# Sample attention rebuilt: a half chunk's softmax inside the next one's keys, its selection penalty as a matmul, and z's tanh in a tile of its own

## The chip, the cores and the metric

The kernel runs on one core of one Trainium2 chip. The metric is device time in microseconds: 939.07 us is the median of three runs of the kernel before (937.36 to 939.32).

## The reference, cut to what matters

One step of a hybrid decoder layer: an input projection, a gated short convolution beside a three-branch sparse attention, and an output projection; once for a prompt of 1024 tokens and once for 8 sample tokens with 2048 cached positions each. All data is float32. The sample attention, which the change rebuilds, is `nsa_block` with one query per sequence:

```python
s_cmp = einsum('bqgnd,bcgd->bqgnc', q, kv_cmp[:, :, 0])          # 64 compressed blocks
p_cmp = masked_softmax(s_cmp, cmp_end <= qp)
o_cmp = einsum('bqgnc,bcgd->bqgnd', p_cmp, kv_cmp[:, :, 1])
imp   = p_cmp summed over the 4 heads of a group, pairs of blocks added
score = where(valid, imp + bonus, -inf)                          # 33 blocks of 64 rows
_, idx = lax.top_k(score, 16)
sel   = sel_blocks[bi, gi, idx]                                  # gathered key and value rows
p_slc = masked_softmax(einsum('bqgnd,bqgkd->bqgnk', q, sel[..., 0, :]), sel_pos <= q_pos)
o_slc = einsum('bqgnk,bqgkd->bqgnd', p_slc, sel[..., 1, :])
p_win = masked_softmax(einsum('bqgnd,bkgd->bqgnk', q, kv_win[:, :, 0]), m_win)   # last 512 rows
o_win = einsum('bqgnk,bkgd->bqgnd', p_win, kv_win[:, :, 1])
o = gate[..., 0:1] * o_cmp + gate[..., 1:2] * o_slc + gate[..., 2:3] * o_win
# mixer_output
attn_branch = o * silu(z_attn)
y = x + concatenate([b_gate * conv_y * silu(z_conv), attn_branch]) @ w_out
```

The kernel does not gather the selected rows. It scores all 2048 cached rows and adds a penalty of -1e30 to those of blocks that were not chosen.

## The kernel before, in words

Each float32 matrix product is made of two or three products on PE, of a value's rounded high part and the rest: `copy(ACT, h, x)` rounds and `sub(DVE or POOL, l, x, h)` takes the rest (these helpers are L75, L76 and L79, and most rows of a trace carry their lines).

After the input projections, two streams run side by side (`merge`, L30, called at L1463). The first is the prompt's attention (`attn_stream`) and then the output projection (`out_stream`: two halves of 512 columns, each of eight token tiles, each tile 24 products of 512 columns). The second is the convolution's projections, the loading of the output weights, the compression of the cached rows (`cmp_stream`: 16 gathers, four accumulations) and the sample attention (`sample_stream`). Each stream yields estimated costs, and `merge` goes on with the one that is behind; `SO = 1.9` stretches those of the output projection. What comes out is arranged once more when the program is built, so instructions of both streams alternate more finely than the yields. On the chip each engine works through its own list in that order.

The sample attention works in half chunks `(c, h)`: a chunk c is 512 rows of each sequence (c = 4 the window, 0 to 3 the cached rows), h is half of the eight sequences. Its parts:

- Preparation (L1072 to L1135): transposed queries into QA and QB, the new rows' keys and values, and their scores `seh`.
- Compressed branch (L1137 to L1153): scores of the compressed blocks, softmax in `Sc`, its scaling (L1150), and its sum over sequences, `im` (L1152). Then the importances on PE (L1155), the top 16 by two rounds of maximum and replacement (L1162, L1163), the penalty `pen` (L1165), and the compressed values (L1172 to L1193).
- `keys(c, h)` (L1198): for four sequences transposes of the keys (L1206), high and low parts `kh`, `kl`, and products into `s` (L1221, L1222), each one tile late.
- `values(c, h)` (L1226): the softmax of the half chunk first: sum of two parts of the scores (L1235), penalty (L1242), maximum (L1246 or L1250), minimum with the old one (L1251), correction (L1252) and exp (L1247 or L1253) with running sums (L1254). Then transposes of it (L1258), and for four sequences high and low parts of the values `vhl` and 16 products (L1278); the result is corrected and added (L1292).
- The loop at the end calls `keys` of the next half chunk, whole, and then `values` of this one.

Tiles `sd` of 512 KB hold keys and values of one sequence's chunk. There are nine; window tiles come by SP (L1090), cached ones by an indirect load from POOL (L1087), asked for when a tile's values have been used.

At the end `sample_half` (L1367) multiplies the sample's rows with the output weights: the convolution's half after each half of the columns, the attention's half when everything else is done, and a write of y_sample (L1431) closes the kernel.

`z_attn` (L695) makes z's SiLU for the prompt's attention, 128 tokens at a time, with its tanh in the buffer `acc` that the convolution uses too (L711).

Of the kernel before, what the change touches and what calls it, by code (L numbers as in the profile page):

```python
# [60 lines left out]
def hymba_step_kernel(ctx, tc, io):  # L61
# [624 lines left out]
    cu = cv.tile([128, 2 + NTOK], F32, name="cu")  # L686
    uo = cv.tile([128, 4, 16], F32, name="uo")
# [7 lines left out]
    def z_attn(a, n):  # L695
        t = cv.tile([128, 512], F32, name="acc")[:, :4 * n].rearrange("p (a c) -> p a c", a=4)
        silu2(mixA[:, :, a:a + n], mixA[:, :, a:a + n], t)

    def conv_use(kind, i, c, o, s):
# [7 lines left out]
        else:  # L707
# [3 lines left out]
            acc = cv.tile([128, 512], F32, name="acc")  # L711
# [15 lines left out]
    def conv_stream():  # L727
        yield from chan
        p = bank("mm")
        for i in range(4):  # L730
            PE.transpose(p[:10, i * 128:(i + 1) * 128], uo[:, i, :10], ident)
        ur = cv.tile([128, 512], F32, name="acc")[:10]
        copy(ACT, ur, p[:10])
        SP.dma_start(io["p_conv"].rearrange("l b r c -> (l b r) c"), ur[0:2])
        SP.dma_start(io["s_conv"].rearrange("l b r c -> (l b) r c")[:, 1, :], ur[2:10])
        yield 400
# [17 lines left out]
    def attn_stream():  # L754
# [147 lines left out]
        for ui, u in enumerate(units):  # L902
            o = [None]
            share = PACE[u[0]]
            if ui % 4 == 2 and u[0] < 7:
                z_attn(u[0] * 128 + 128, 128)
            elif ui == 3:
                z_attn(SEQ, 8)
# [5 lines left out]
            for br, P in ((1, P1), (2, P2)):  # L914
# [25 lines left out]
                if ui == 0 and br == 1:  # L940
                    z_attn(0, 128)
# [30 lines left out]
    def cmp_stream():  # L972
# [95 lines left out]

    def sample_stream():
        sp_ = ctx.enter_context(pool("smp", "right"))  # L1070
        small = sp_.tile([64, 112], F32, name="small")
        SP.dma_start(small, io["c_small"])  # L1072
        mext, bonus, Gsel = small[:, 0:8], small[:, 8:48], small[:, 48:112]
        QA = sp_.tile([128, 2, 8, 8], F32R, name="QA")
        QB = [sp_.tile([128, 32, 8], F32R, name=f"QB{h}") for h in range(2)]
        POOL.memset(f(QA), 0.0)
        ptz = [sp_.tile([128, 4, 32, 8], F32R, name=f"ptz{h}") for h in range(2)]
        for h in range(2):
            POOL.memset(f(QB[h]), 0.0)
            POOL.memset(f(ptz[h]), 0.0)  # L1080
# [14 lines left out]
        for _ in range(NSD):  # L1095
            load(*next(ahead))


        p = bank("pt")
        qg = sp_.tile([8, 4, 2, 64], F32, name="qg", tag="st")  # L1100
        copy(DVE, qg, q_s.rearrange("p (g h d) -> p h g d", g=2, h=4))
        for h in range(4):
            PE.transpose(p[:, h * 8:h * 8 + 8], qg[:, h].rearrange("p g d -> p (g d)"), ident[:8, :8])
        for g in range(2):
            q = slice(g * 64, g * 64 + 64)
            pv = p[q, :32].rearrange("p (h b) -> p b h", h=4)
            copy(ACT, QA[q, 0, :, g * 4:g * 4 + 4], pv)
            sub(DVE, QA[q, 1, :, g * 4:g * 4 + 4], pv, f(QA[q, 0, :, g * 4:g * 4 + 4]))
        for h in range(2):
            for i in range(2):  # L1110
                copy(DVE, QB[h][:, 4 * i:4 * i + 28:9, :], f(QA[:, i, 4 * h:4 * h + 4]))
        QAf = QA.rearrange("p i b r -> p (i b r)")
        yield 600

        p = bank("pt")
        for i in range(2):
            PE.transpose(p[:, i * 8:i * 8 + 8], srows[1 + i][:, 0:128], ident[:8, :8])
        kn = sp_.tile([128, 2, 16], F32R, name="kn")
        copy(ACT, kn[:, 0], p[:, :16])
        sub(DVE, kn[:, 1], p[:, :16], f(kn[:, 0]))  # L1120
        vn = sp_.tile([8, 2, 2, 128], F32R, name="vn")
        for i in range(2):
            copy(ACT, vn[:, i, 0], srows[1 + i][:, 128:256])
            sub(DVE, vn[:, i, 1], srows[1 + i][:, 128:256], f(vn[:, i, 0]))
        p = bank("pt")
        PE.matmul(p[:, :16], QAf, kn[:, 0], start=True, stop=False)
        PE.matmul(p[:, :16], QAf, kn[:, 1], start=False, stop=True)
        se = sp_.tile([64, 2, 8], F32, name="se")
        copy(ACT, se, p[64:128, :16].rearrange("p (i b) -> p i b", i=2))
        DVE.tensor_tensor(se, p[0:64, :16].rearrange("p (i b) -> p i b", i=2), se, OP.add)  # L1130
        DVE.tensor_tensor(se, se, mext[:, None, :].to_broadcast([64, 2, 8]), OP.add)
        seh = sp_.tile([32, 2, 2, 8], F32, name="seh")
        for h in range(2):
            copy(ACT, seh[:, h], se[32 * h:32 * h + 32])
        yield 600  # L1135
# [224 lines left out]
    def out_stream():  # L1360
# [65 lines left out]
        while 8 not in done:  # L1426
            yield None
# [97 lines left out]
```

## Time and profile before

| | |
|---|---|
| runs, median (lowest to highest) | 939.07 us (937.36 to 939.32) |
| profiled execution | 939.33 us, span 937.6 us |
| PE busy | 873.8 us, 93% of the span |
| DVE busy | 619.4 us, 66% |
| ACT busy | 556.0 us, 59% |
| POOL busy | 404.3 us, 43% |
| bytes moved by DMA | 82.24 MB, 88 GB/s on average |

PE multiplies matrices, DVE, ACT and POOL are the vector, scalar and GpSimd engines, SP issues most transfers. A row of a group of instructions names line, engine, operation, the tile written and the tiles read, their shapes and the count; then the busy time in us, the mean of one in ns, and the idle time of the engine before them with what ended it. In a row of the timeline the first two numbers are start and duration in us, and a bracket at the end holds the idle time before it and what ended that. The chain of waits puts 49% of the span on PE, 7% each on ACT and DVE, 3% on POOL.

### The profile page before, as it was taken

The page shows a single profiled execution, that of the slowest core. Times are in us where ns is not written, and L with a number is a line of the kernel's source. Part 1 is how long each engine was busy: PE and PEld are TensorE (multiplying, and loading weights), DVE is VectorE, ACT ScalarE, POOL GpSimd, SP SyncE. Part 2 cuts the span into 40 slices and gives each one's busy share as a digit, 9 for nine tenths or more (in the row PEclk, how much of TensorE's full clock was granted, in tenths as well). Part 3 has the DMA queues.
Part 4 walks back from the last instruction along what each step waited for, and adds up shares of the span by engine and source line. Part 5 has one row for each costly group of instructions (what it writes and reads, how often), then busy time and mean ns, then how long its engine had stood idle before and what let it go on. Part 6 is the DMA issues. An engine that isn't in the chain of part 4 may idle for free.

```text
span 937.6 us, 16976 instructions
## 1 busy us (share of the span) xinstructions
PE 873.8 (93%) x5789; PEld 783.2 (84%) x5789; DVE 619.4 (66%) x1714; ACT 556.0 (59%) x1495; POOL 404.3 (43%) x550
## 2 busy tenths in 40 slices
PE   7988999999899999999989999999679999798998
PEld 6888999999689889898979899998568888576765
DVE  5896734788655555856775686577745555877883
ACT  5764543733665655656556666576757666675761
POOL 4132340311454444444434444343455543477761
PEclk8999989999999999999999999999989999899999
DMA  7513331211011000000000100001495661857631
GB/s 246 154 57 95 95 114 35 80 57 31 6 30 34 24 23 24 23 24 23 13 12 23 24 23 1 23 2 44 127 302 182 214 214 47 314 179 226 214 102 47
DMA packets 57955, 82.24 MB, mean 88 GB/s; under 512 B 14470, under 2 KB 43086, under 8 KB 55692
## 3 DMA queue, kind: packets, MB, share of 16 engines
q1 hardware_dynamic: 50956, 47.60, 16.9%
q0 software_dynamic: 6912, 33.56, 10.6%
q8 instruction: 46, 0.75, 0.3%
q14 instruction: 41, 0.34, 0.1%
HBM read 74.24 MB, written 11.10 MB: 91 GB/s over the span
## 4 chain that ended last, share of the span: by engine, by line
PE 49%; ACT 7%; DVE 7%; POOL 3%; issue 3%; DMA 1%; ACTq 0%; DVEq 0%; POOLq 0%
PE o L880 7%; PE pt L870 5%; PE s L796 5%; PE mm L225 5%; PE mm L224 5%; PE mm L223 5%; POOL P L845 2%; ACT P L786 2%; PE mm L1407 1%; PE pt L999 1%; PE mm L1405 1%; PE mm L1406 1%; PE mm L1023 1%; ACT ph L75 1%; PE o L1278 1%
## 5 line engine op out<-in xcount | busy, mean ns | idle before, releaser
L223 PE MATMUL mm<-hH,wh 128*128 128x384 f32 (+1 forms) x480 | 157.9, 329 | 0.0
L225 PE MATMUL mm<-hH,wl 128*128 128x384 f32 (+1 forms) x480 | 155.7, 324 | 0.0
L224 PE MATMUL mm<-hL,wh 128*128 128x384 f32 (+1 forms) x480 | 155.1, 323 | 0.0
L786 ACT ACTIVATE P<-P,stat 128x640 f32<-128x640 f32 (+7 forms) x192 | 112.9, 590 | 37.4 <-DVE stat L784 36.8
L79 POOL TENSOR_TENSOR wl<-wraw,wh 128x256 fp32r<-128x256 f32 (+1 forms) x120 | 87.7, 749 | 106.2 <-ACT wh L75 96.8
L79 DVE TENSOR_TENSOR pl<-pt,ph 128x512 fp32r<-128x512 f32 (+1 forms) x164 | 102.4, 636 | 45.3 <-ACT ph L75 43.9
L75 ACT ACTIVATE ph<-pt 128x512 fp32r<-128x512 f32 (+1 forms) x164 | 88.3, 549 | 66.1 <-PE pt L870 65.5
L845 POOL TENSOR_SCALAR P<-P,stat,gates 128x640 f32<-128x640 f32 (+7 forms) x128 | 101.1, 800 | 55.8 <-DVE stat L836 52.7
L870 PE MATMUL pt<-ident,P 128*128 128x128 f32 x592 | 95.5, 278 | 6.4 <-POOL P L845 3.5
L796 PE MATMUL s<-k,q 128*128 128x320 f32 (+8 forms) x416 | 95.8, 334 | 3.7 <-DVE q L79 1.5
L208 PE MATMUL mm<-wh,hH 128*128 128x256 f32 (+1 forms) x320 | 93.5, 292 | 0.4 <-ACT hH L75 0.4
L209 PE MATMUL mm<-wl,hH 128*128 128x256 f32 (+1 forms) x320 | 93.2, 292 | 0.2
L210 PE MATMUL mm<-wh,hL 128*128 128x256 f32 (+1 forms) x320 | 93.0, 291 | 0.0
L223 PEld LDWEIGHTS mm<-hH,wh 128*128 128x128 f32 x480 | 91.9, 191 | 0.8 <-DVE mixC L693 0.6
L224 PEld LDWEIGHTS mm<-hL,wh 128*128 128x128 f32 x480 | 91.9, 191 | 0.1
L225 PEld LDWEIGHTS mm<-hH,wl 128*128 128x128 f32 x480 | 91.9, 192 | 0.1
L784 DVE CUSTOM_DVE_ANT_0 P<-s,mask 128x32 f32<-128x32 f32 (+8 forms) x160 | 70.9, 473 | 27.0 <-PE s L796 22.4
L870 PEld LDWEIGHTS pt<-ident,P 128*128 128x128 f32 x592 | 70.0, 140 | 19.9 <-POOL P L845 10.1
L880 PE MATMUL o<-ph,v 128*128 128x256 f32 x264 | 74.5, 301 | 3.6 <-ACT ph L75 3.0
L880 PE MATMUL o<-pl,v 128*128 128x256 f32 x264 | 73.3, 300 | 3.3 <-DVE pl L79 3.2
L796 PEld LDWEIGHTS s<-k,q 128*128 128x128 f32 x416 | 66.8, 190 | 8.1 <-DVE q L79 1.7
L841 POOL TENSOR_SCALAR P<-P,stat,gates 128x32 f32<-128x32 f32 x64 | 22.9, 370 | 94.4 <-DVE stat L836 76.4
(342 smaller groups left out, 2182.9 us busy)
## 6 DMA issues: line engine op xcount, KB each, us to landing
wraw<-in_w_in_dram SPq DMA_DIRECT2D x56, 256.0 KB
xt<-in_x_prompt_dram SPq DMA_DIRECT2D x8, 512.0 KB
wor<-in_w_out_dram SPq DMA_DIRECT2D x16, 256.0 KB
xr<-in_x_prompt_dram SPq DMA_DIRECT2D x16, 256.0 KB
out_y_prompt_dram<-xr SPq DMA_DIRECT2D x16, 256.0 KB
sd<-in_state_win_kv_dram SPq DMA_DIRECT2D x8, 512.0 KB
out_s_win_dram<-in_state_win_kv_dram SPq DMA_DIRECT2D x8, 511.0 KB
cwr<-in_cmp_w_dram SPq DMA_DIRECT2D x32, 64.0 KB
```

The costliest lines, as they stand in the source:

```text
L75: return ACT.activation(out, in_, AF.Copy)
L79: return eng.tensor_tensor(out, a, b, OP.subtract)
L208: PE.matmul(o[:, :n], hH[t // 3][:, k, s], wh, start=k == 0, stop=False)
L209: PE.matmul(o[:, :n], hH[t // 3][:, k, s], wl, start=False, stop=False)
L223: PE.matmul(o[:, :n], wh, hH[c][:, k], start=k == 0, stop=False)
L224: PE.matmul(o[:, :n], wh, hL[c][:, k], start=False, stop=False)
L225: PE.matmul(o[:, :n], wl, hH[c][:, k], start=False, stop=k == 7)
L786: return lambda: ACT.activation(P, P, AF.Exp, bias=stt[:, 0, c:c + 1], scale=-1.0, accum_out=stt[:, 1, c:c + 1])
L796: PE.matmul(s[:, a:b], q[:, i], k, start=first, stop=not first)
L845: POOL.tensor_scalar(P[:, i, :n], P[:, i, :n], stt[:, 2, c + i:c + i + 1], gates[:, qi, gt:gt + 1], op0=OP.mult, op1=OP.mult)
L870: PE.transpose(p[:, y * 256 + i * 128:y * 256 + i * 128 + 128], src[:, i], ident)
L880: PE.matmul(o[0][:, :256], v, X[:, y * 256:y * 256 + 256], start=br == 1 and x == 0 and y == 0 and X is h[0], stop=last and y + 1 == len(p ...
```

## The change

The change has these parts:

- `sample_start` is new: the preparation of queries, new rows and `seh` (now negated, with its minimum) runs inside the compression, after gathers 4, 7 and 10, in a pool of its own. POOL copies the queries there. Two tiles are new: `penx`, the penalty spread over a chunk, and `pick`, which selects half of its rows.
- Compressed branch: `im` is reduced before the scaling; ACT scales `im`, POOL scales `Sc` with sum and gate in one operation. The keys of the first half chunk come before the importances' product. The compressed values (`compressed`) come after the first half chunk's softmax.
- Keys: a product may now be two tiles late, with three buffers; the penalty of a selected chunk is added by one more product into `s`, `penx` by `pick` (L1191 of the kernel after).
- Softmax (`weigh`, new): sum, negation and maximum in one DVE operation; the corrections for both parts of the result and the running sum on ACT. It is called in the middle of the next half chunk's keys, after their second tile.
- Values: the correction and addition read the result from PSUM in one operation for both parts; the parts are added at the end.
- The end: the sample's output products are placed inside the second half of the output projection, two token tiles after the sample attention is done, or at the end if it is not. `SO` is 1.95. The first four weight pieces of the second half are split by POOL, not DVE.
- `z_attn` takes 64 tokens at a time and has a tile of its own, `zt`; `acc` is 384 wide instead of 512.

```diff
     def z_attn(a, n):
-        t = cv.tile([128, 512], F32, name="acc")[:, :4 * n].rearrange("p (a c) -> p a c", a=4)
+        t = zt[:, :4 * n].rearrange("p (a c) -> p a c", a=4)
...
-            if ui % 4 == 2 and u[0] < 7:
-                z_attn(u[0] * 128 + 128, 128)
-            elif ui == 3:
+            if ui % 4 > 1 and u[0] < 7:
+                z_attn(u[0] * 128 + ui % 2 * 64 + 128, 64)
+            elif ui == 1:
                 z_attn(SEQ, 8)
...
+        start = sample_start(cp)
         for n in range(16):
...
+            if n in (4, 7, 10):
+                next(start, None)
...
+                products(2)
+                if b % 4 == 1 and between:
+                    between()
                 yield 870
...
+            if b == 3 and c < 4:
+                PE.matmul(s[:64], pick[:, 64 - 64 * h:128 - 64 * h], penx, start=False, stop=True)
...
+        im = sp_.tile([64, 64], F32, name="im")
+        DVE.tensor_reduce(im, Sc.rearrange("p (b c) -> p c b", b=8), axis=AX, op=OP.add)
         DVE.tensor_scalar(stt[:, 1:2], stt[:, 1:2], 1e-30, None, op0=OP.max)
         DVE.reciprocal(stt[:, 2:3], stt[:, 1:2])
-        DVE.tensor_scalar(Sc, Sc, stt[:, 2:3], None, op0=OP.mult)
-        im = sp_.tile([64, 64], F32, name="im")
-        DVE.tensor_reduce(im, Sc.rearrange("p (b c) -> p c b", b=8), axis=AX, op=OP.add)
+        ACT.activation(im, im, AF.Copy, scale=stt[:, 2:3])
+        POOL.tensor_scalar(Sc, Sc, stt[:, 2:3], gr[:, 0:1], op0=OP.mult, op1=OP.mult)
         yield 450
+        yield from keys(*steps[0])
+        products(0)
...
-            DVE.tensor_tensor(Sb[:, :512], s[0:32], t, OP.add)
-                DVE.tensor_tensor(v, v, penh[:, h][:, None, :, None].to_broadcast([32, 4, 32, 4]), OP.add)
-                DVE.tensor_reduce(nm, Sb[:, :w], axis=AX, op=OP.max, negate=True)
+            DVE.tensor_tensor_reduce(Sb[:, :512], s[0:32], t, scale=-1.0, scalar=1e30, op0=OP.add, op1=OP.min, accum_out=nm)
...
                 DVE.tensor_tensor(nm, nm, old, OP.min)
-                ACT.activation(al, old, AF.Exp, bias=nm, scale=-1.0)
-                DVE.scalar_tensor_tensor(su, su, al, cs, op0=OP.mult, op1=OP.add)
+                for i in range(2):
+                    ACT.activation(fac[32 * i:32 * i + 32, h, br:br + 1], old, AF.Exp, bias=nm, scale=-1.0)
+                ACT.activation(su, su, AF.Identity, bias=cs, scale=fac[0:32, h, br:br + 1])
...
-                t = sp_.tile([32, 256], F32, name="ot")
-                rows_sum(o, t, 32)
-                DVE.scalar_tensor_tensor(acc[:, h, 1], acc[:, h, 1], al, t, op0=OP.mult, op1=OP.add)
+                DVE.scalar_tensor_tensor(a, a, fac[:, h, br:br + 1], o[:64, :256], op0=OP.mult, op1=OP.add)
...
         for i, u in enumerate(steps):
-            if i + 1 < len(steps):
-                yield from keys(*steps[i + 1])
-            yield from values(*u)
+            if 0 < i < len(steps) - 1:
+                got = []
+                yield from keys(*steps[i + 1], lambda u=u, got=got: got.append(weigh(*u)))
+                Sb = got[0]
+            else:
+                Sb = weigh(*u)
+                yield 100
+            if i == 0:
+                yield from compressed()
+            elif i + 1 == len(steps):
+                yield 4000
+            yield from values(*u, Sb)
...
-                    late.pop(0)()
+                    late.pop(0)(POOL)
...
-    SC, SO, SM2, SS = 1.0, 1.9, 1.0, 1.0
+    SC, SO, SM2, SS = 1.0, 1.95, 1.0, 1.0
```

How the lists of two engines change shows at three places. On PE at the sample stage's start, before, from the compressed scores (kcH, kcL) to the importances (`pt<-im`, L1155) and the first keys' products (`s<-kh`, `s<-kl`); `om` and `mm` are output tiles:

```order
L1138 MATMUL s<-kcH,QA 128x512
L1139 MATMUL s<-kcL,QA 128x512
L1206 MATMUL ptx<-ident,sd 128x128 x4
L1406 MATMUL om<-wol_10622,mh 128x512
L1407 MATMUL om<-woh_10621,ml 128x512
L1155 MATMUL pt<-im,small 64x64
L1173 MATMUL pt<-ident,Sb 128x64 x4
L1206 MATMUL pt<-ident,sd 128x128 x4
L1221 MATMUL s<-kh,QB_10378 64x512
```

And now, PE at the importances' product (L1216), from the third key tile's transposes (L1169) on:

```order
L1169 MATMUL ptx<-ident,sd 128x128 x4
L1187 MATMUL s<-kh,QB_9456 64x512
L1188 MATMUL s<-kl,QB_9456 64x512
L1465 MATMUL om<-wol_10714,mh 128x512
L1466 MATMUL om<-woh_10713,ml 128x512
L1187 MATMUL s<-kh,QB_9456 64x512
L1169 MATMUL pt<-ident,sd 128x128 x4
L1188 MATMUL s<-kl,QB_9456 64x512
L1216 MATMUL pt<-im,small 64x64
```

The importances' product moved from behind one key tile to behind four; the compressed scores (L1196, L1197) stand some 35 rows ahead of it.

On PE at the first values, before: from the transposes of the first softmax (`pt<-ident,Sb`) to the first selected chunk's keys:

```order
L1258 MATMUL pt<-ident,Sb 128x32 x4
L1265 MATMUL ptx<-ident,Sb 8x32
L1206 MATMUL pt<-ident,sd 128x128 x4
L1405 MATMUL om<-woh_9977,mh 128x512
L1406 MATMUL om<-wol_9978,mh 128x512
L1278 MATMUL o<-vhl,ptz_10381 64x256 x16
L1286 MATMUL o<-vn,pte 64x256
```

And now the same place, where `sd` at L1169 are tiles of the first selected chunk and L1315 the value products:

```order
L1187 MATMUL s<-kh,QB_9457 64x512
L1188 MATMUL s<-kl,QB_9457 64x512
L1302 MATMUL ptx<-ident,Sb 8x32
L1464 MATMUL om<-woh_10719,mh 128x512
L1247 MATMUL o<-vcHL,ptc 128x256 x4
L1169 MATMUL pt<-ident,sd 128x128 x8
L1169 MATMUL ptx<-ident,sd 128x128 x3
L1315 MATMUL o<-vhl,ptz_10448 64x256 x16
```

Eleven transposes instead of four stand ahead of the first sixteen value products.

On POOL at the sample stage's start, before: from the tiles cleared there (QA, QB, ptz) to the first indirect loads (`sd<-in_cache_slc_kv`):

```order
L1080 MEMSET ptz_10382 128x1024
L79 TENSOR_TENSOR ml<-mixA,mh 128x512
L79 TENSOR_TENSOR vhl<-sd,vhl 128x4x128 x2
L1169 TENSOR_SCALAR Sb<-Sb,gr 64x512
L1087 DMA sd<-in_cache_slc_kv_dram,idx_s 128x1024 x5
L79 TENSOR_TENSOR ml<-mixC,mh 128x512
```

And now, with the low parts of the output weights (`wol`) among them:

```order
L1159 MEMSET ptz_10449 128x1024
L79 TENSOR_TENSOR wol_10708<-wor,woh_10707 128x512
L79 TENSOR_TENSOR wol_10714<-wor,woh_10713 128x512
L79 TENSOR_TENSOR ml<-mixC,mh 128x512
L1211 TENSOR_SCALAR Sb<-Sb,cst_10459,gr 64x512
L79 TENSOR_TENSOR ml<-mixA,mh 128x512
L79 TENSOR_TENSOR vhl<-sd,vhl 128x4x128 x2
L1147 DMA sd<-in_cache_slc_kv_dram,idx_s 128x1024 x5
L79 TENSOR_TENSOR wol_10720<-wor,woh_10719 128x512
```

Two weight subtractions and one more of an output tile come ahead of the first indirect loads; the scaling of the softmax moved ahead of the value subtractions.

## Rows read from the trace of the kernel before

**Rows 1.** Busy us (count) by stretch: PE, PEld, DVE, ACT, POOL; clock, DMA share, GB/s.

```profile
240.00:648.00 408.00, 395.94 (x2655) 364.89 (x2656) 260.87 (x767) 251.35 (x707) 183.25 (x300) 1.00 0.08 19
702.00:796.00 94.00, 91.95 (x615) 80.54 (x615) 48.86 (x87) 63.54 (x123) 42.31 (x53) 1.00 0.50 169
796.00:812.00 16.00, 10.47 (x51) 6.72 (x50) 13.77 (x42) 8.79 (x26) 8.76 (x8) 0.79 0.85 320
812.00:850.00 38.00, 37.35 (x222) 27.13 (x220) 29.84 (x60) 28.09 (x59) 25.30 (x22) 1.00 0.61 210
850.00:870.00 20.00, 17.45 (x100) 13.22 (x99) 15.88 (x24) 12.07 (x26) 12.65 (x12) 0.91 0.64 210
870.00:913.00 43.00, 40.30 (x236) 31.00 (x235) 34.75 (x71) 29.78 (x64) 31.69 (x26) 1.00 0.49 162
913.00:933.00 20.00, 20.00 (x94) 14.03 (x92) 8.99 (x19) 3.22 (x9) 5.10 (x5) 1.00 0.14 53
```

**Rows 2.** The same view over two low clocks and the load's peak.

```profile
800.00:804.00 4.00, 2.24 (x10) 1.20 (x10) 3.96 (x14) 2.98 (x8) 0.89 (x1) 1.00 1.02 413
804.00:811.00 7.00, 3.79 (x16) 2.96 (x17) 5.05 (x17) 2.91 (x8) 6.20 (x6) 0.52 0.87 303
862.00:866.00 4.00, 4.00 (x15) 2.59 (x13) 1.15 (x3) 1.22 (x2) 0.09 (x2) 0.57 0.47 153
```

**Rows 3.** Waits of PE from 795 us on: us in total, times, longest.

```profile
PE pt L1155 <- DVE im L1152: 4.3, 1, 4.3
PE s L1222 <- DVE kl L79: 2.8, 3, 2.1
PE s L1221 <- ACT kh L75: 1.5, 1, 1.5
PE pt L1258 <- ACT Sb L1253: 0.8, 1, 0.8
```

**Rows 4.** Timeline of DVE and PE at the importances.

```profile
805.03 0.76 DVE L1150 TENSOR_SCALAR Sb<-Sb,cst 64x512 f32<-64x512 f32 x1
805.82 1.02 DVE L1152 TENSOR_REDUCE im<-Sb 64x64 f32<-64x512 f32 x1
806.89 0.47 PE L1155 MATMUL pt<-im,small 64*64 64x64 f32 x2 [4.30 <-DVE im L1152]
```

**Rows 5.** Timeline of DVE, POOL and PE around 860 us.

```profile
857.92 3.02 DVE L1254 SCALAR_TENSOR_TENSOR stats<-stats 32x1 f32<-32x1 f32 x1
858.42 1.30 POOL L79 TENSOR_TENSOR vhl<-sd,vhl 128x512 fp32r<-128x512 f32 x1
859.66 1.27 POOL L79 TENSOR_TENSOR ml<-mixC,mh 128x512 fp32r<-128x512 f32 x1
861.61 0.45 PE L1222 MATMUL s<-kl,QB 128*64 128x512 f32 x1 [2.14 <-DVE kl L79]
```

**Rows 6.** Groups of DVE, 795 to 938 us, by shape.

```profile
L1242 DVE TENSOR_TENSOR Sb<-Sb,penh 32x512 f32<-32x512 f32 x8 | 9.2, 1151 | 0.0
L1235 DVE TENSOR_TENSOR Sb<-s,st 32x512 f32<-32x512 f32 x10 | 6.8, 677 | 9.8 <-ACT st L75 9.8
L1254 DVE SCALAR_TENSOR_TENSOR stats<-stats 32x1 f32<-32x1 f32 x6 | 4.1, 680 | 0.0
```

**Rows 7.** Indirect loads of `sd` and POOL's subtractions: timeline, group, landing, durations.

```profile
807.79 1.05 POOL L1087 DMA_INDIRECT sd<-in_cache_slc_kv_dram,idx_s  x1 [0.17 <-issue]
L1087 POOL DMA_INDIRECT sd<-in_cache_slc_kv_dram,idx_s x32 | 33.9, 1061 | 8.4 <-issue 4.0 <-PE pt L1206 0.9 <-POOL vhl L79 0.8
DMA to landing us min/median/max: 5.1/5.6/6.9
L79 POOL TENSOR_TENSOR vhl<-sd,vhl x20: 1290/1308/2390, 803.1 to 912.5; 128x512 fp32r<-128x512 f32 x20
```

**Rows 8.** Timeline of SP at the end.

```profile
934.55 0.30 SPq L1431 DMA_DIRECT2D out_y_sample_dram<-y  x1
```

**Rows 9.** The tanh of z by the tile `acc`: count, ns min/median/max, first and last start.

```profile
L692 ACT ACTIVATE acc<-mixA x9: 230/622/632, 237.1 to 562.5; 128x512 f32<-128x512 f32 x8, 128x32 f32<-128x32 f32 x1
```

More of the change, by code (lines that the diff above doesn't have):

```diff
@@ L731, in conv_stream @@
             PE.transpose(p[:10, i * 128:(i + 1) * 128], uo[:, i, :10], ident)
[L732 to L735, printed above, removed]
+        for a in range(2):
+            c = slice(a * 256, a * 256 + 256)
+            ur = cv.tile([128, CH], F32, name="acc")[:10, :256] if a else zt[:10]
+            copy(ACT, ur, p[:10, c])
+            SP.dma_start(io["p_conv"].rearrange("l b r c -> (l b r) c")[:, c], ur[0:2])
+            SP.dma_start(io["s_conv"].rearrange("l b r c -> (l b) r c")[:, 1, c], ur[2:10])
         yield 400
@@ L1096, in sample_stream @@
             load(*next(ahead))
[L1099 to L1108, printed above, removed]
@@ L1109, in sample_stream @@
-        for h in range(2):
[L1110 to L1135, printed above, removed]
+        ptz = [sp_.tile([128, 4, 32, 8], F32R, name=f"ptz{h}") for h in range(2)]
+        for h in range(2):
+            POOL.memset(f(ptz[h]), 0.0)
+        sums, pend = {}, []
@@ new lines, in keys @@
+        def keys(c, h, between=None):
+            s = sums[c, h] = bank("s")
+            for b in range(4 * h, 4 * h + 4):
+                r = tiles[c, b].rearrange("p (t j c) -> p t j c", t=4, j=2)
+                p = bank("pt")
+                for t in range(4):
+                    PE.transpose(p[:, t * 128:(t + 1) * 128], r[:, t, 0], ident)
+                kh = sp_.tile([128, 512], F32R, name="kh", bufs=3)
+                kl = sp_.tile([128, 512], F32R, name="kl", bufs=3)
+                copy(ACT, kh, p)
+                sub(DVE, kl, p, f(kh))
+                pend.append((s, c, h, b % 4, kh, kl))
+                products(2)
+                if b % 4 == 1 and between:
+                    between()
+                yield 870
@@ new lines, in products, with product @@
+        def products(n):
+            while len(pend) > n:
+                product(*pend.pop(0))
+        def product(s, c, h, b, kh, kl):
+            q = QB[h][:, b * 8:(b + 1) * 8].rearrange("p i r -> p (i r)")
+            PE.matmul(s[:64], q, kh, start=b == 0, stop=False)
+            PE.matmul(s[:64], q, kl, start=False, stop=b == 3 and c == 4)
+            if b == 3 and c < 4:
+                PE.matmul(s[:64], pick[:, 64 - 64 * h:128 - 64 * h], penx, start=False, stop=True)
+        steps = [(c, h) for c in (4, 0, 1, 2, 3) for h in range(2)]
@@ L1165, in sample_stream @@
         DVE.tensor_scalar(pen, sc[:, 0:32], BIG / 10, BIG, op0=OP.is_gt, op1=OP.mult)
[L1166 to L1169 removed]
+        copy(ACT, penx[0:64].rearrange("p (t n r) -> p t n r", t=4, r=4),
+             pen[:, None, :, None].to_broadcast([64, 4, 32, 4]))
         yield 100
[L1171 to L1173 removed]
@@ L1383, in out_stream, with sample_end @@
             yield None
+        def sample_end():
+            for n in range(2):
+                sample_half(n, 1)
+                yield 1700
+            SP.dma_start(y_sample, y8)
         late = []
+        over = 0
         for n in range(2):
```

227 lines of the change are left out of this document (132 added, 95 removed).

## The prediction, made before the result was known

> **What bounds the kernel now.** I read the slices of the page first: PE is busy 93% of the span and its digit is 9 nearly everywhere, so the kernel is a queue of matmuls, and a change is worth what it takes out of PE's idle time or puts into its work. Next the busy time by stretch [rows 1], to find where PE is not full. The long attention and convolution stretch (240 to 648 us) has 12 us of idle PE in 408. The compression stretch (702 to 796) has 2.05 in 94. The sample attention that follows is worse: 5.53 idle of 16 at its start, then 0.65 of 38, 2.55 of 20 and 2.70 of 43; after 913 PE is full again with the last output tiles. So the stage that the change rebuilds holds 11.4 us of idle PE. Then the same view over the places where the clock digit falls [rows 2]: 804 to 811 ran at a mean 0.52 and 862 to 866 at 0.57. These follow the two longest idle times. Half clock costs only while PE works: 3.79 us busy at 0.52 would have taken about 2.0 at full, so 1.8 lost; 4.00 at 0.57 would have taken 2.3, so 1.7 lost. At stake in all: 5.5 + 1.8 = 7.3 at the start and 5.9 + 1.7 = 7.6 after it.
>
> Who ended the waits [rows 3]: 4.3 us for the reduced block importances (L1152), 2.8 for the low halves of the keys on DVE, 1.5 for their high halves on ACT, 0.8 for a finished softmax. Two of them explain themselves. L1155 stands in PE's list behind only a few products, while its operand comes through a scaling and a 1.02 us reduction on DVE [rows 4]; PE, which works its list in order, sat still. And the 2.14 us before 861.61 [rows 5]: a one-column operation, L1254, held DVE for 3.02 us, and the subtraction for the keys stood behind it. It ended when POOL's two subtractions, 858.42 to 860.93, ended; its six instances average 0.68 us, far above what one column needs.
>
> [...]
>
> **The change part by part.** The sum is made against the profiled execution, 939.33 us (span 937.6, 1.7 around it); the runs' median is 939.07.
>
> *Start of the sample stage, 7.3 at stake.* The queries' and new rows' preparation moves into compression, and the importances are reduced before the scaling, which goes to ACT and POOL. More important is the place: in PE's new list between the scores' last product and L1216 stand four tiles' transposes, six key products and 23 output products, where L1155 stood behind one tile and two output products. The 27 added wide products are 6.5 us at 0.24 each (priced below), and the scaling of 0.76 us [rows 4] is off the path: more than the 4.3 us. So this wait goes, and with it, I expect, the low clock. What is late next: in the new list eleven transposes of the first selected chunk stand ahead of sixteen value products. Their tiles come by POOL's indirect loads, issued after POOL's share of the first values, now with two weight subtractions ahead. A load takes 5.6 us from issue to landing and the next is issued about 1.06 + 8.4/32 = 1.3 us later [rows 7], so the third lands some 8 us after the first issue, at 807.79 before. PE has 88 instructions from the stage's beginning at 796 to there, at the 0.17 us of 870 to 913 (40.30 us for 236 [rows 1]) 15 us, so it gets there at 811, and the third tile lands at 807.8 + 2.6 + 5.6 = 816 if POOL keeps its time. Bounds: 0, since POOL's first load came behind the scaling that waited with PE and may come 4 us sooner; 5, if the two extra subtractions (1.3 us each, 2.4 at the worst [rows 7]) use that up. I take the middle, 2.4. Term: -7.3 + 2.4 = **-4.9**, bounds -7.3 and -2.3.
>
> *The half chunks, 7.6 at stake.* For each of the eight half chunks of selected keys DVE loses the penalty addition (L1242, 1.15 us), the separate maximum, a copy and L1254; addition, negation and maximum become one operation with one input in PSUM, priced by L1235 at 0.68 [rows 6]. Over ten half chunks DVE gives up 9.2 + 4.1 + the ten maxima (6.8, at L1235's 0.68 each) = 20 us, and some more with the value accumulation that now reads PSUM directly; ACT gets a few one-column operations. DVE was busy 80.5 of the 101 us from 812 to 913 [rows 1], so by this it falls to about 60%. The softmax now runs while the next keys' last two tiles are transposed, so PE has products to do meanwhile. Not all idle time goes: kh still waits for ACT, and each list is fixed in advance. I take two thirds: **-5.0**, bounds -7.6 and -2.5.
>
> *The penalty as a matmul.* Eight extra 64x512 products on PE. From 913 to 933 PE did 94 products in 20.00 us, that is 0.21, with some narrower ones among them; I take 0.24: **+1.9**. Nothing hides it, since PE is the bound; bounds 1.7 and 2.3.
>
> *Compression.* It takes eight small PE instructions with their POOL, ACT and DVE work, and loses filler: in the new order one of its four accumulations has only the eight products of a sample half beside it, where before it had a whole output tile. PE's total is not changed by that, but alone the chain gather, regroup, transpose, split, product may not fill PE. The trace shows no such stretch. Bounds: -1.0 (half of the 2.05 idle there) and +2.6 (the idle share of the worst neighbour, 2.55 of 20, over one accumulation of some 20 us). I take **+0.8**, nearer to the full stretch.
>
> *Weight pieces on POOL.* Four subtractions of 0.67 leave DVE; POOL was idle 26% to 45% of each stretch from 796 to 913 [rows 1], so the cost is the queueing counted at the start. 0 beyond that.
>
> *The end.* The sample's output products move ahead of the last two tiles. Before, after PE's last product came two additions of about 0.68 and a 32 KB write issued at 934.55 [rows 8]; now one addition, and a 256 KB write. At 413 GB/s [rows 2] the larger write needs 0.55 more. **-0.2**, bounds -0.7 and +0.5. PE keeps 48 products behind the sample's last result, so its final chain stays covered.
>
> *z's tanh.* Nine tanh of 0.62 us become seventeen, sixteen of them half as wide, and they no longer share the convolution's one buffer. ACT and DVE gain some 1 us each in 408 us in which they are busy 62% and 64% [rows 1, 9]; the waits that the shared buffer caused ended on those engines, not on PE. **0**, bounds -1.5 and +1.5.
>
> Sum: 939.3 - 4.9 - 5.0 + 1.9 + 0.8 - 0.2 = 931.9 us, 0.8% below the median. All low bounds together give 924, all high bounds 941.
>
> **The rivals.** *All of the idle time goes.* The DVE relief and the cover are enough to fill PE as it is filled from 913 on: 939.3 - 7.3 - 7.6 + 1.9 - 0.2 = 926. For it: DVE's load in [rows 1]; against it: the loads at the start and ACT, at 60% to 74% busy, which copies every tile twice.
>
> *The gain goes into the loads.* The first selected chunk is waited for in full (5 us), PE's clock falls again and takes 1.8, and with a faster stage each later chunk's tiles come 0.5 us late in eight half chunks: 939.3 - 4.9 - 5.0 + 1.9 + 0.8 - 0.2 + (5 - 2.4) + 1.8 + 4 = 940, no change. For it: an 8 us path from issue to the third landing; against it: after the start the DMA share is 0.49 to 0.64.
>
> *Slower: the softmax returns in front of the keys.* The transposes of a finished softmax now stand ahead of the next half chunk's last key products in PE's list, so a late softmax stops the keys as well. Small operations of its chain have moved onto ACT, where they queue behind the tile copies in order. Before, such a wait showed 0.8 us [rows 3]. If the eight half chunks that are weighed amid keys wait w each and the half chunk term is lost, the time is 939.3 - 4.9 + 1.9 + 0.8 - 0.2 + 8w: slower than before from w = 0.3, and 943 at 0.8. Against it: between the last product that a softmax needs and its transposes stand, in the new list, sixteen value products, sixteen transposes and some dozen wide products; the last alone are 2.9 us at 0.24, and the chain's three wide steps about 0.7 each, priced by L1235.
>
> *The rebuilt order elsewhere.* Every engine's list after 240 us is arranged anew, and 12 us of small waits there may come out 3 us either way; this is in the bounds.
>
> **How the numbers follow.** Forecast 931.9, own range 927 to 936: 0.60. All idle gone, 926: 0.17. Gain lost in the loads, 936 to 941: 0.13. Softmax in front of the keys, 941 to 945: 0.10. What this kernel's runs can tell apart is about 0.2%, 1.9 us. Faster takes the first two and a third of the loads' case, 0.81; same 0.08; slower 0.11. The range for 8 in 10 leaves out the lower half of the second case and the upper end of the others: 924.5 to 939.
>
> **What would show it.** Right: the wait at the importances is gone, no clock below full in the middle of the stage, DVE's busy time there down by over 20 us, and PE idle some 4 us instead of 11.4. A wait of PE for tiles of the first selected chunk, of 2 to 3 us, is the price I set; 5 or more with a low clock is the second rival. Waits before the softmax transposes in most half chunks are the third. Wrong at the root would be a longer compression stretch or idle time of PE in attention by more than 3 us.

## The result and the profile after

The changed kernel takes **943.3 us** (median of five runs, 942.98 to 945.13) against 939.07 for the kernel before (five runs, 936.58 to 940.38): ratio 1.0057, 95% interval 1.0039 to 1.0074. It is slower by 0.6%. The forecast was 931.9 with a range of 924.5 to 939.

The stage that was rebuilt runs from the last product of compression to the end. First the busy time of it in the kernel before, then in the changed one (columns as in [rows 1]):

```profile
795.70:937.60 141.90, 125.95 (x695) 92.35 (x695) 104.89 (x215) 82.24 (x182) 83.49 (x69) 0.96 0.52 179
```

```profile
797.20:941.30 144.10, 128.40 (x704) 94.76 (x704) 85.83 (x166) 85.66 (x195) 87.80 (x76) 0.99 0.52 175
```

VectorE was relieved as forecast: 104.9 to 85.8 us, 19.1 less. TensorE's idle time did not move: 141.9 - 125.95 = 15.95 us before, 144.1 - 128.4 = 15.7 after. It is also busy for longer, although the clock is higher. What it waits for is different. The waits of TensorE from 797 us on (us in total, times, longest), against [rows 3]:

```profile
PE s L1188 <- DVE kl L79: 6.4, 8, 2.1
PE s L1187 <- ACT kh L75: 2.3, 4, 1.4
PE o L1315 <- DVE ptz L79: 0.9, 1, 0.9
PE s L1187 <- ACT penx L75: 0.9, 1, 0.9
```

The 4.3 us for the importances are gone, as forecast. The waits for the keys' low halves `kl`, 2.8 us before, are now 6.4, although the engine that computes them has less to do. The reason stands in the timelines around the three longest: GpSimd, VectorE, and TensorE's wait that followed.

```profile
805.18 1.29 POOL L79 TENSOR_TENSOR ml<-mixA,mh 128x512 fp32r<-128x512 f32 x1
806.45 2.50 POOL L79 TENSOR_TENSOR vhl<-sd,vhl 128x512 fp32r<-128x512 f32 x2
806.30 3.19 DVE L79 TENSOR_TENSOR vhl<-sd,vhl 128x512 fp32r<-128x512 f32 x1
809.42 0.68 DVE L79 TENSOR_TENSOR kl<-ptx,kh 128x512 fp32r<-128x512 f32 x1
810.15 0.44 PE L1188 MATMUL s<-kl,QB 128*64 128x512 f32 x1 [2.11 <-DVE kl L79]
...
825.25 0.96 POOL L1147 DMA_INDIRECT sd<-in_cache_slc_kv_dram,idx_s  x1 [3.24 <-DVE acc L1358]
826.24 1.28 POOL L79 TENSOR_TENSOR vhl<-sd,vhl 128x512 fp32r<-128x512 f32 x1
825.60 2.48 DVE L79 TENSOR_TENSOR vhl<-sd,vhl 128x512 fp32r<-128x512 f32 x1 [0.36 <-ACT vhl L75]
828.73 0.44 PE L1188 MATMUL s<-kl,QB 128*64 128x512 f32 x1 [1.25 <-DVE kl L79]
...
845.30 0.94 POOL L1147 DMA_INDIRECT sd<-in_cache_slc_kv_dram,idx_s  x1 [0.30 <-issue]
846.26 2.52 POOL L79 TENSOR_TENSOR vhl<-sd,vhl 128x512 fp32r<-128x512 f32 x2
846.42 2.92 DVE L79 TENSOR_TENSOR vhl<-sd,vhl 128x512 fp32r<-128x512 f32 x1 [2.19 <-ACT vhl L75]
850.00 0.45 PE L1188 MATMUL s<-kl,QB 128*64 128x512 f32 x1 [1.00 <-DVE kl L79]
```

These are the subtractions for the values' low halves, which the code hands to VectorE and GpSimd in turn. With GpSimd free of subtractions one takes VectorE 0.67 to 0.69 us (e8 below). Here it takes 3.19, 2.48 and 2.92, and each time it ends some 0.55 us after GpSimd's run of work (809.49 against 808.95, 828.08 against 827.52, 849.34 against 848.78): each was held until that run was over. The keys' subtraction stands behind it in VectorE's list, and TensorE behind that: 2.11, 1.25 and 1.00 us. The second wait was followed by half clock:

```profile
830.00:833.50 3.50, 3.50 (x16) 3.06 (x15) 1.44 (x4) 2.09 (x4) 1.83 (x2) 0.51 0.81 255
```

One difference of the two traces lies ahead of the rebuilt stage. The changed kernel's attention starts at half clock for 10.3 us, the kernel before for 3.4, and every later point of attention is some 3 us later:

```profile
239.50:249.80 10.30, 9.15 (x31) 8.10 (x32) 5.95 (x31) 5.63 (x23) 2.69 (x6) 0.50 0.01 2
```

The change is not needed for it: e5, e15 and e17 below work through the same lists as the kernel before up to 680 us, and show 10.2, 6.8 and 6.8 us of it. The other kernels, faster ones among them, lie between 3.4 and 10.2 too.

### The profile page after: what moved, and what is told of

It reads as the page before. It is cut to its first block, busy times and chain, and to the rows that moved or that the text cites. A ratio compares the mean times of both kernels' runs of the same rounds, so it can differ in the third digit from the quotient of the medians.

```text
span 941.3 us, 16976 instructions
## 1 busy us (share of the span) xinstructions
PE 879.3 (93%) x5797; PEld 787.4 (84%) x5797; DVE 607.2 (65%) x1687; ACT 561.5 (60%) x1524; POOL 408.2 (43%) x559
## 4 chain that ended last, share of the span: by engine, by line
PE 46%; ACT 9%; DVE 7%; issue 3%; POOL 3%; DMA 2%; SPq 0%; ACTq 0%; DVEq 0%; POOLq 0%
PE o L883 7%; PE pt L873 5%; PE s L799 5%; PE mm L225 5%; PE mm L224 5%; PE mm L223 5%; ACT P L789 2%; PE pt L1002 1%; PE om L1026 1%; DMA wor<-in_w_out_dram 1%; ACT ph L75 1%; PE om L1464 1%; PE om L1466 1%; PE om L1465 1%; PE mm L1026 1%
```

## The experiments

Ratios are to the kernel before, timed beside it on the same chip, with a 95% interval.

**First four: which part.** The edits, in this order:

```
e1: the kernel before, with the change's lines of z_attn, conv_use's acc, conv_stream and attn_stream
e2: the changed kernel, with those lines as before
e3: -  sub((DVE, POOL)[b % 2], vhl[:, :, 1], v, f(vhl[:, :, 0]))
    +  sub(DVE, vhl[:, :, 1], v, f(vhl[:, :, 0]))
e4: -  late.pop(0)(POOL)
    +  late.pop(0)()
```

> The kernel before with only z's edit (tanh in a tile of its own, pieces of 64 and at other units, the conv rows copied out in two halves). Theory 1, the smaller pieces at the first unit hold TensorE at half clock longer (239.5 to 249.8 us in the trace after, 241.0 to 244.4 before, and every later marker of attention is 2.3 to 3.3 us late): about 942, with the half clock near 240 us lasting some 10 us again. Rival, how long the clock stays low there does not depend on z's pieces: 939, within 1.5.

> The changed kernel with z's edit undone. Theory 1: about 940 (943.3 less 3.3). Rival (not z): 943, within 1.5. In neither case more than 1 us of change after the last compressed row.

> The changed kernel with all the subtractions for the values' low halves on VectorE; before they alternate between VectorE and GpSimd. Theory 2, the stage's gain was lost where a VectorE subtraction with both inputs in SBUF ran beside GpSimd's (3.19 us at 806.30, 2.48 at 825.60, 2.92 at 846.42, instead of 0.68) and the keys' low halves stood behind it (TensorE idle 2.1 + 1.25 + 1.0 us and the half clock from 830.0 to 833.5, 1.7): these three go, 943.3 - 4.35 - 1.7 = 937, and no such subtraction is above 1.5 us except beside GpSimd's subtractions of the output's rows. Rival, VectorE gets 20 more subtractions of 0.68 = 13.6 us and the keys' low halves come late all the same: 943 or more.

> The changed kernel with the four weight pieces' subtractions back on VectorE. Theory 2: GpSimd reaches its two subtractions of the values about 3 us sooner, no longer together with VectorE's at 806.30, so the wait of 2.1 us at 810 shrinks or goes: 941 to 943. Rival, the weight pieces have no part in it: 943.3, within 1.

e1: 939.24, ratio 1.0003 (0.9985 to 1.0021), and its low clock lasted from 241.9 to 248.7 us. Theory 1 falls: z's edit costs nothing, to within 1.7 us. e2: 1.0040 (1.0024 to 1.0057), which overlaps the changed kernel's own interval.

e3: **933.57, ratio 0.9933** (0.9909 to 0.9957), nearly 10 us from one line. VectorE got 13.6 us of work (twenty subtractions at 0.68), and TensorE waits less for it. VectorE's busy time in the stage rose by only 1.05 us (86.88 against 85.83), so by estimate some 12.5 us of what counted as its busy time in the changed kernel was time in which it was held. The stage and TensorE's waits in e3:

```profile
800.30:934.60 134.30, 125.29 (x704) 93.64 (x704) 86.88 (x186) 84.99 (x195) 65.94 (x56) 1.00 0.55 187
```

```profile
PE s L1188 <- DVE kl L79: 1.9, 3, 0.9
PE s L1187 <- ACT kh L75: 1.5, 5, 0.4
PE ptx L1169 <- DMA sd<-in_cache_slc_kv_dram,idx_s: 0.7, 1, 0.7
```

Idle time is 9.0 us instead of 15.7. I had expected 937, counting the three waits only. Others went with them, such as 1.38 us for `kh` at 900.95 and 0.94 for `ptz` at 914.57; whether these too came from a held operation was not followed. e4: 1.0039 (1.0015 to 1.0063). Without the weight pieces GpSimd still had an output tile's subtraction and two of values in a row, and VectorE's took 3.23 us; that part of my expectation was wrong, and the weight pieces cost nothing that can be measured.

**Next four: is the edit good without the rebuild, and what are the terms worth.** All but e5 start from e3:

```
e5: the kernel before, with e3's line
e6: -  if b == 3 and c < 4:
    -      PE.matmul(s[:64], pick[:, 64 - 64 * h:128 - 64 * h], penx, start=False, stop=True)
e7: -  yield from keys(*steps[i + 1], lambda u=u, got=got: got.append(weigh(*u)))
    +  yield from keys(*steps[i + 1])
    +  products(0)
    +  yield 430
    +  got.append(weigh(*u))
e8: e4's line, and
    -  sub(POOL, ml, src[:, :, s], f(mh))
    +  sub(DVE, ml, src[:, :, s], f(mh))
```

> The kernel before with all the subtractions for the values' low halves on VectorE. It tells what the same edit is worth without the rebuild. Theory 2, the rebuild had the gain that was forecast and lost it where VectorE and GpSimd met: the kernel before meets less (TensorE waits 2.14 us at 861.61 and runs at half clock there, 1.7), and its VectorE is fuller (80.5 us of 101), so the edit brings at most 3.8 and may cost: 936 to 941, and the changed kernel with the edit (933.6) stays the faster. Rival, the edit is good in any case and the rebuild by itself costs time: about 930, 9 less, as in the changed kernel.

> The changed kernel with the values' low halves on VectorE, and without the eight products that add the penalty (it leaves the penalty on unselected blocks out of the sums). Forecast's term +1.9 for eight products at 0.24 us: 933.6 - 1.9 = 931.7. Rival, TensorE would otherwise have waited in those places, so the products cost nothing: 933.6, within 1.

> The changed kernel with the values' low halves on VectorE, and each half chunk's softmax after the next one's keys, as in the kernel before, in place of amid them. The forecast's half chunk term had two parts, VectorE's relief and the cover. If the cover carries it: waits of TensorE at the softmax's transposes of 0.5 to 0.9 us in most half chunks, 936 to 939. If the relief alone carries it: 933.6, within 1.

> The changed kernel with all low halves (values, weight pieces, output rows) on VectorE, so that GpSimd subtracts nothing after attention. Theory 2 for what is left: VectorE's 1.65 us subtraction at 808.48 and TensorE's waits of 0.9 and 0.7 around it go: 932, within 1.5. Rival, VectorE, which gets some 36 more subtractions of 0.68, is late for the keys: 936 or more.

e5: 934.85, ratio 0.9962 (0.9934 to 0.9989). The kernel before gains too, 3.4 us, where the changed one gains nearly 10: the meetings cost it less, but the 3.02 us of [rows 5] was one. That the changed kernel with the edit is the faster of the two, as I expected, is not shown: the intervals of e3 and e5 overlap. e6: 930.93, 0.9920 (0.9892 to 0.9948). The times of e3 and e6 can't be told apart, but TensorE's busy time in the stage is 1.83 us less (123.46 against 125.29), so the eight products have about their price of 1.9. e7: 935.11, 0.9983 (0.9962 to 1.0003): the cover is worth something, 1.5 us by the medians and 4.7 by the ratios. The waits that I expected at the softmax's transposes did not come, but for one of 0.8 us for `ptz`; those for `kl` and `kh` grew by some 0.5 each. e8: 930.80, 0.9918 (0.9893 to 0.9942). With GpSimd free of subtractions in the stage, no 128x512 subtraction on VectorE for the values or the output rows takes over 0.71 us there (e8, ns min/median/max):

```profile
L79 DVE TENSOR_TENSOR vhl<-sd,vhl x40: 670/675/694, 798.3 to 898.0; 128x512 fp32r<-128x512 f32 x40
L79 DVE TENSOR_TENSOR ml<-mixA,mh x8: 661/681/710, 806.9 to 920.9; 128x512 fp32r<-128x512 f32 x8
```

**Next four: GpSimd's reading or its fullness, and the end.**

```
e9:  e3, and behind its line
     +  if b % 2: sub(POOL, <the used keys' half of r>, v, f(vhl[:, :, 0]))
e10: e3, and behind its line
     +  if b % 2: POOL.memset(<the same half>, 0.0), twice
e11: e8, with  sub(DVE if n == 0 or t < 5 else POOL, ml, src[:, :, s], f(mh))
e12: e3, with  sample_half(n, 0); yield 1700  behind each column's tiles, and sample_end() last
```

> The changed kernel with the values' low halves on VectorE, and beside it twenty subtractions on GpSimd with the same two inputs, in the places where the changed kernel has GpSimd's; their result goes to a part of the loaded tile that nobody reads again. Nobody waits for them but GpSimd's own next loads. Theory 2 (VectorE is held up while GpSimd reads SBUF): VectorE's subtractions of 2 to 3 us are back, and with them TensorE's waits for the keys' low halves: 940 to 946. Rival, the values waited for GpSimd's slower results (1.29 us against 0.68), and that is what the edit removed: 933.6, within 1.5.

> The same with two 128x512 memsets in place of each of those subtractions (some 1 us for both, by the 0.95 that one of 128x1024 took at 797.6): GpSimd is as full, but reads no SBUF. Theory 2: 933.6, within 1.5, VectorE's longest subtraction under 1.7 us. Rival, GpSimd's fullness, by which loads are issued late, is the cost: as the run with the subtractions, 938 or more.

> All low halves on VectorE, as in the run with 930.8, but for the output rows of the last three tiles, which stay on GpSimd. In that run TensorE waited 1.98 us at 909.17 for the sample's output rows, which stood behind such subtractions on VectorE, and its clock fell from 910.3 to 913.7 (1.7): if these are the price, 930.8 - 3.7 = 927; at least 929 if the wait only moves.

> The changed kernel with the values' low halves on VectorE, and the sample's output halves and its write where the kernel before has them (halves behind each column's tiles, the last two and the write at the very end). Forecast's term for the end, -0.2: 933.8, within 1. Rival, from the two traces: the new end brings TensorE 1.0 us of waits (at 913.75 and 915.65) and saves 0.7 behind its last product, and eight tiles' compression has a sample half for a filler where it had whole tiles; without it 931 to 932.

e9: 944.38, **1.0048** (1.0031 to 1.0066). Work on GpSimd whose result nobody uses brings the whole loss back, so it was not the values waiting for a slower engine. VectorE's long subtractions are back too:

```profile
L79 DVE TENSOR_TENSOR vhl<-sd,vhl x40: 671/682/2871, 802.0 to 908.4; 128x512 fp32r<-128x512 f32 x40
```

e10: 936.76, 0.9980 (0.9959 to 1.0001), between the two, and its trace shows why it does not decide: GpSimd still had its output subtractions, and they now met a VectorE operation, `acc` times `fac`, that takes 0.34 us in the changed kernel (e10, GpSimd and VectorE):

```profile
830.73 0.94 POOL L1147 DMA_INDIRECT sd<-in_cache_slc_kv_dram,idx_s  x1 [0.30 <-PE o L1327]
831.69 1.29 POOL L79 TENSOR_TENSOR ml<-mixC,mh 128x512 fp32r<-128x512 f32 x1
832.93 1.27 POOL L79 TENSOR_TENSOR ml<-mixA,mh 128x512 fp32r<-128x512 f32 x1
831.08 3.27 DVE L1361 TENSOR_SCALAR acc<-acc,fac 64x256 f32<-64x256 f32 x1
```

e12: 938.67, 1.0003 (0.9977 to 1.0028), which missed both expectations, in part for the same reason: that operation took 3.13 us at 830.18, and TensorE waited 2.2 us at 833.96; it also waited 1.9 us for a window's rows at 800.51. e11: 930.35, 0.9901 (0.9866 to 0.9936); the wait of 1.98 us at 909 went, but not the time, so that expectation was too good.

**The last five**, on a base without subtractions on GpSimd:

```
e13: e8, and e10's two memsets
e14: e8, and e9's subtraction
e15: the kernel before, with e3's line and e8's for ml
e16: e8, and e12's edit
e17: e15, and
     -  DVE.tensor_scalar(Sc, Sc, stt[:, 2:3], None, op0=OP.mult)
     (the reduction to im moves ahead of the reciprocal)
     +  ACT.activation(im, im, AF.Copy, scale=stt[:, 2:3])
     +  POOL.tensor_scalar(Sc, Sc, stt[:, 2:3], gr[:, 0:1], op0=OP.mult, op1=OP.mult)
        yield 450
     +  yield from keys(*steps[0])   # no longer behind the compressed values
     (POOL's own scaling of Sc by the gate, further down, goes)
```

> The changed kernel with all low halves on VectorE (930.8, ratio 0.992), and two 128x512 memsets on GpSimd for every second tile of values (20 pairs, some 1 us each), to a part that nobody reads again. GpSimd is fuller and issues its loads later, but reads no data from SBUF. Theory 2: ratio 0.990 to 0.994, no VectorE subtraction of 128x512 over 1.5 us. Rival (GpSimd's fullness): 0.997 or more.

> The same with one 128x512 subtraction (two SBUF inputs, 1.29 us) on GpSimd in place of each pair of memsets; nobody uses its result. Theory 2: VectorE's subtractions of 1.3 to 3 us are back, ratio 0.996 to 1.002. Rival: as the memsets within 0.002.

> The kernel before with all low halves on VectorE. If the rebuild is worth what the forecast's terms say (-7.1 of 939), this kernel lies at 930.8 + 7.1 = 938 (ratio 0.999 or so). If the kernel before too lost only to such meetings: 932 or less (ratio 0.993 or less), and the rebuild by itself is worth nothing. I expect between the two: its VectorE was busy 105 of 141 us after compression, and some 11 more with the output rows' subtractions (16 at 0.68) and 13.6 with the values' would fill 130 of 141: ratio 0.997, 936.

> The changed kernel with all low halves on VectorE, with the sample's output halves and write where the kernel before has them. Forecast's term for the end, -0.2: ratio 0.992, within 0.0015. Rival 1, the wait of 1.98 us at 909.17 and the half clock behind it go with it: 0.988. Rival 2, as in the run e12 the changed order of the output tiles costs in other places: 0.996 or more.

> The kernel before with all low halves on VectorE (929.8, ratio 0.990), and of the rebuild only the start: the importances are reduced before the scaling, which goes to ScalarE and GpSimd, and the first half chunk's keys stand ahead of their product. The forecast's mechanism: the wait of 5.33 us (and 0.68 behind it) and the half clock that follows it go, small waits for the keys come in their place as in the changed kernel with all low halves on VectorE (3.7 us lost from the last compressed row to the first value product, against 9.1): 929.8 - 5.4 = 924.4, ratio 0.985, within 0.002. Rival, the wait only moves (the keys wait for VectorE, which is busy with the 64x512 steps): 928 to 931, ratio 0.988 or more.

e13: 0.9943 (0.9923 to 0.9963). e14: 0.9991 (0.9973 to 1.0009). The intervals do not touch. With memsets VectorE's subtractions are nearly as short as without (0.74 us at most, 0.71 in e8); in e13 six of the 56 (`vhl` and `ml`) overlap a memset, and none of the six takes over 0.69 us. With subtractions on GpSimd three are long again, one of `vhl` and two of `ml`. The row of `vhl` in e13, then `vhl` and `ml` in e14:

```profile
L79 DVE TENSOR_TENSOR vhl<-sd,vhl x40: 669/675/695, 796.6 to 898.9; 128x512 fp32r<-128x512 f32 x40
```

```profile
L79 DVE TENSOR_TENSOR vhl<-sd,vhl x40: 669/675/2424, 798.0 to 904.2; 128x512 fp32r<-128x512 f32 x40
L79 DVE TENSOR_TENSOR ml<-mixC,mh x8: 674/692/1867, 796.8 to 922.6; 128x512 fp32r<-128x512 f32 x8
L79 DVE TENSOR_TENSOR ml<-mixA,mh x8: 662/680/2155, 806.6 to 925.5; 128x512 fp32r<-128x512 f32 x8
```

So most of the loss comes with GpSimd's subtractions, which read two tiles, and not with its memsets, which read none: of the step from e8 (0.9918) to e14 (0.9991), about two thirds lies between memsets and subtractions. The two do not fill GpSimd quite alike (busy 58.4 us in the stage of e13, 70.1 in e14). `vhl` takes 0.70 us at most with memsets, up to 2.42 with subtractions.

e15: **929.78, 0.9903** (0.9882 to 0.9923). The kernel before, with GpSimd relieved in the same way, is as fast as the changed kernel in e8 (0.9918). e16: 929.82, 0.9911 (0.9884 to 0.9939), within 1 us of e8: the new end has no worth that can be measured, as forecast.

e15 still has the wait at the importances, with half clock behind it. Its longest waits and the low stretch:

```profile
PE pt L1155 <- DVE im L1152: 5.3, 1, 5.3
PE ptx L1206 <- DMA sd<-in_cache_slc_kv_dram,idx_s: 1.3, 2, 1.1
```

```profile
800.30:810.50 10.20, 7.02 (x28) 5.49 (x29) 6.68 (x20) 3.90 (x10) 4.52 (x5) 0.50 0.87 292
```

e17 does that one part of the rebuild: **925.53, 0.9857** (0.9825 to 0.9889), the fastest version, 1.4% under the kernel before and, by the two ratios, 2% under the changed one. The wait is gone, and from 796 to 812 the clock is full:

```profile
796.00:812.00 16.00, 12.35 (x65) 7.28 (x64) 14.86 (x40) 13.10 (x30) 5.65 (x5) 1.00 0.90 321
```

## Why the prediction was wrong

The step that failed is what the forecast made of the 3.02 us of [rows 5]. It saw that L1254 was over when GpSimd's two subtractions were, booked the 4.1 us of L1254 as work that VectorE gives up, and put no term for such meetings in the changed kernel into its sum. They cost that kernel nearly 10 us (e3). The victims were others there. Four of the one-column minima were indeed held in the changed kernel, 1.24 to 1.28 us instead of 0.14, but TensorE's three longest waits for `kl` stand behind the values' 128x512 subtractions, twenty of which stay on VectorE beside twenty on GpSimd, as before, and which the forecast did not look at. In the trace of before the longest of them was 1.41 us, with the same line of code: what differs in the traces is the moment at which the two engines meet. The change moved every list, and three then stood beside GpSimd's work for 2.48 to 3.19 us.

Nor was L1254 the only operation held before. The penalty addition L1242 stands in [rows 6] with a mean of 1.15 us, and I took that for its work. Four of its eight instances took 1.20 to 1.78 us beside GpSimd's subtractions; with GpSimd relieved each takes 0.67. Its row before, then in e15:

```profile
L1242 DVE TENSOR_TENSOR Sb<-Sb,penh x8: 670/937/1776, 833.6 to 907.9; 32x512 f32<-32x512 f32 x8
```

```profile
L1242 DVE TENSOR_TENSOR Sb<-Sb,penh x8: 671/671/677, 830.8 to 901.9; 32x512 f32<-32x512 f32 x8
```

With L1254 (0.68 against 0.20), half of the 13.3 us that these two gave to VectorE's relief was time in which VectorE was held, not work.

- **Start, -4.9.** Right in mechanism: e17 against e15 is -4.3, with intervals that overlap by little. That the size fits too is in part luck. I took 2.4 off for loads, and in the changed kernel none of TensorE's waits in this stage is for a transfer; in e17 they are 0.7 us. In the changed kernel the wait was replaced by those for `kl` at 804.91 (0.91) and 810.15 (2.11) and for the penalty at 814.86 (0.93).
- **Half chunks, -5.0.** VectorE's busy time fell as forecast (19.1 us, forecast 20), but VectorE's fullness was not what made the keys late. In e15 it is busy 111.7 of 138.9 us, more than before, and no wait for `kl` is left among TensorE's seven longest. Between the first and the last value product TensorE idles (span less busy time) 91.70 - 86.45 = 5.25 us before and 94.80 - 88.73 = 6.07 after; without GpSimd's subtractions 3.34 in e15 and 1.00 in e8. On that base the rebuild is worth 2.3 us there, just outside the bound of -2.5. The four stretches, in this order:

```profile
823.40:915.10 91.70, 86.45 (x511) 65.88 (x510) 72.91 (x138) 62.05 (x132) 67.53 (x55) 0.98 0.56 184
```

```profile
821.60:916.40 94.80, 88.73 (x519) 67.53 (x519) 60.17 (x111) 64.81 (x147) 64.65 (x56) 0.98 0.54 175
```

```profile
820.60:908.10 87.50, 84.16 (x512) 64.85 (x511) 77.27 (x163) 61.09 (x131) 29.42 (x27) 1.00 0.60 194
```

```profile
815.20:902.20 87.00, 86.00 (x523) 66.41 (x522) 66.84 (x141) 64.54 (x148) 29.46 (x27) 1.00 0.58 191
```

- **Penalty, +1.9.** About right (1.83 us of TensorE's busy time, e6 against e3).
- **Weights on GpSimd, 0; end, -0.2; z, 0.** Within what can be measured (e4, e16, e1).
- **Compression, +0.8.** Not tested alone. From the first transpose to the last product it took 108.6 us against 110.0, of which 1.7 are a half clock at 698 us that only the kernel before had there.

The prediction's sum of all low bounds is off by a little: with z's -1.5 it is 922.9, not 924.

Of the rivals, the slower one named 941 to 945. That the time falls there is luck, for the mechanism is another: it had TensorE waiting at the softmax's transposes, and the changed kernel's list of waits has only one of the softmax's, 0.9 us for `ptz`. None of the rivals has what happened, VectorE's subtractions held beside GpSimd's.

The time came about as follows. The changed kernel's span is 3.7 us longer in the traces (941.3 against 937.6). Compression begins 2.9 us later, about what the longer half clock at the start of attention costs:

```profile
L999 PE MATMUL pt<-ident,reg x172: 270/272/421, 685.7 to 790.5; 128*128 128x128 f32 x172
```

```profile
L1002 PE MATMUL pt<-ident,reg x172: 270/272/330, 688.6 to 792.2; 128*128 128x128 f32 x172
```

From there to the end it takes 252.7 us against 251.9, where the forecast's terms add up to a gain of 7.4. Of the rebuild's gain at the start and in the half chunks, the held operations took back all (idle 15.95 against 15.7), and the penalty's products came on top. The 2.45 us more of busy time in the stage are not these products alone, for some 17 more of the output projection's products stand in the changed kernel's stage than in the stage of before. How much of the 4.2 us between the medians is attention's scatter stays open.

That the whole rebuild is worth nothing over e15 is not settled either. From compression's first transposes to the end e8 takes 239.3 us and e15 243.4, but these transposes start 3.9 us later in e8. Half clock at the start of attention, 10.2 us against 6.8, is some 1.7 of that; z's edit, which e8 has and e15 has not, could be in the rest. The intervals allow anything from 3 us better to 6 worse. e8 also has a new wait of 1.98 us with half clock behind it; in e11 it is gone, and the time is the same within its interval.

## What to carry to other kernels

When an engine is late, look at the longest instance of each of its operations beside the median before counting its busy time: here subtractions of 3.19, 2.92 and 2.48 us beside a median of 0.68 were held up, and 19.1 us less on VectorE left TensorE's idle time where it was (15.7 us, 15.95 before). Two engines that took a step's tiles in turn were a hazard here that the reordering rolled anew: the longest of these subtractions on VectorE was 1.41 us before it and 3.19 after. Taking GpSimd, the slower of the two (1.29 us against 0.68), off that work brought 0.4% to 1.2% here for one line. And test the parts of a rebuild alone, on a base where the hazard is gone: here one part alone brought 0.5% where the whole brought nothing that can be measured.

## What the runs showed of the hardware

- A VectorE subtraction was held for several GpSimd subtractions in a row: in the changed kernel one that began at 806.30, during one of GpSimd's, lasted through two more (3.19 us). It is not always so: in the kernel before, L1242 at 907.93 (1.78 us) ended 0.54 us after the first of two GpSimd subtractions in a row, and the second took 1.72 us instead of 1.3.
- A VectorE operation that began before GpSimd's subtraction could still end after it: in the changed kernel at 825.60, 0.64 us ahead (2.48 us), and in [rows 5], 0.50 us ahead (3.02 us), both while GpSimd was issuing an indirect load. With such issues and no subtractions beside it, in e15, no subtraction of the values took over 0.75 us.
- An operation with one SBUF tensor, `acc` times `fac` (0.34 us), was held as well: 3.27 us in e10 and 3.13 in e12 beside GpSimd's subtractions, and 2.42 in e13 beside memsets and the issue of a load alone. In e13:

```profile
829.94 0.94 POOL L1147 DMA_INDIRECT sd<-in_cache_slc_kv_dram,idx_s  x1 [0.30 <-issue]
830.88 1.00 POOL L1315 MEMSET sd<- 128x512 f32 x2
831.80 1.01 POOL L1316 MEMSET sd<- 128x512 f32 x2
830.53 2.42 DVE L1361 TENSOR_SCALAR acc<-acc,fac 64x256 f32<-64x256 f32 x1
```

- In e15 a wait cost twice: 5.33 us, and behind it 7.02 us of work at a granted clock of 0.50, by estimate some 3.5 more. In e17, without that wait, the clock is 1.00 from 796 to 812.
